# Hybrid encoder trunk: token-side sums in two portions, second product over all six blocks of a part

## Chip, cores, metric

One core of one Trainium2 chip runs the whole program. The metric is the device time of one execution in microseconds; the figure compared is the median over the runs of a kernel. The engines are named as in the profile: PE (matmul), PEld (its weight loads), DVE (VectorE), ACT (ScalarE), POOL (GpSimd) and SP, whose queue issues the loads.

## What is computed

Two layers of an encoder over 512 tokens with 1024 channels, in float32. Each layer runs a half-step feed-forward block, a mixer, a cross attention and a second half-step feed-forward block, each added to the residual x. The change touches only the feed-forward block, which therefore runs four times:

```
def swiglu(x, w_in, w_out):            # w_in 1024 x 5632, w_out 2816 x 1024
    gate, up = jnp.split(x @ w_in, 2, axis=-1)
    return (jax.nn.silu(gate) * up) @ w_out
...
x = x + 0.5 * swiglu(rms_norm(x, norm_ffn1[l]), ffn1_wi[l], ffn1_wo[l])
```

## The kernel before

Channels lie on the 128 partitions and the 512 tokens (T) along a row, so x is eight tiles of 128x512 (called x, or xs later in the program). Precision is kept by writing every matmul operand as a high and a low part: `split` makes the high part on ACT (an ACTIVATE copy) and the low part on DVE (source minus high), and `mm3` issues three matmuls, hi·hi, hi·lo and lo·hi. Names ending in hi and lo are such pairs: h (the normed input), w (weights of a plain product), s (weights of a Strassen-like product), t (sums of the input over tokens), f (hidden values).

The function `ffn` walks over 22 blocks f of 128 hidden channels. They are grouped by PARTS into four parts: f = 0 to 3, 4 to 9, 10 to 15 and 16 to 21.

- `plain(f)` (f = 0 to 3) makes gate and up with 24 matmuls of 512 columns each, into the PSUM tiles pg and pu. Its weights come through two `raw` buffers and three `whi`/`wlo` buffers of 512 columns; one such half feeds 12 matmuls.
- `seven(f)` (f from 4) makes the same with seven products of 12 matmuls of 256 columns, into PSUM tiles named p. In the order of issue they are 1, 2, 6, 3, 7, 5, 4. Products 1, 2 and 3 use h; 6, 7, 5 and 4 use sums of h over token halves and channel halves. The weight side needs sums of its own, made on DVE (`ws`), then split into `shi`/`slo` (seven buffers).
- `token_sums` makes the token-side sums once per feed-forward block, before any `seven`: for each of four channel pairs k one scaled copy on ACT (b), four DVE instructions on 256 columns (s), and two splits (thi on ACT, tlo on DVE).
- `second(f0, f1, ...)` is the second product (@ w_out) of a part that is finished: for each of eight output tiles, 12 or 18 matmuls of 512 columns into `po`, then two DVE instructions that add it to x. Its weights are loaded into `wr` and split into the same `whi`/`wlo` buffers. It is a generator and is advanced from inside the next part: each of the seven yields of a `seven` adds WO_RATE to a credit that starts at minus WO_LEAD, and each whole credit advances `second` by one step (24 steps for the first part, 32 for a later one). What is left is run at the end of the part. The last part's second product runs alone.

The order on each engine is made by a scheduler that follows program order where it can but lets an instruction go ahead when, by its own planning, an earlier one is not ready. After that each engine runs its instructions strictly in the order given.

Of the kernel before, what the change touches and what calls it, by code (L numbers as in the profile page):

```python
# [8 lines left out]
F32 = mybir.dt.float32  # L9
# [5 lines left out]
P = 128  # L15
# [15 lines left out]
REL_MAX = 256  # L31
LEAD, DENSE_RATE, ATT_RATE = 15, (1.0, 0.61, 0.98), 0.65
TURN_RATE = (0.5, 0.9)
PARTS, PLAIN, WO_RATE, WO_LEAD = (0, 4, 10, 16, 22), 4, 1.0, 4

PAR = {}
_n = 0
# [17 lines left out]
def trunk(tc, I, out, depth=DEPTH):  # L55
    nc = tc.nc
    ctx = ExitStack()
    with ctx:
# [13 lines left out]
        def stt(o, a, s, b, op0, op1):  # L72
            nc.vector.scalar_tensor_tensor(out=o, in0=a, scalar=s, in1=b, op0=op0, op1=op1)  # L73

        def act(o, i, f, **k):
            nc.scalar.activation(out=o, in_=i, func=f, **k)  # L76
# [4 lines left out]
        def t2(name, shape=None, dt=F32):  # L81
            return tp.tile(shape or [P, T], dt, tag="t", name=name, bufs=8)
# [45 lines left out]
        def pc(l, n, j=0):  # L128
            o, w = PAR[n]
            return par[:, l, o + j:o + j + 1]  # L130
# [10 lines left out]
        def split(o_hi, o_lo, src):  # L141
            act(o_hi, src, AF.Copy)
            tt(o_lo, src, o_hi.bitcast(F32), sub)
# [123 lines left out]
        def ffn(l, which):  # L267
            h = norm(l, f"norm_{which}")
            wi, wo = I[f"{which}_wi"][l], I[f"{which}_wo"][l]
            with tc.tile_pool(name="hid", bufs=1) as hidp:  # L270
# [10 lines left out]
                def plain(f):  # L281
                    nonlocal r
                    pg = bank(ROT[2 * f % 8], "pg")
                    proj(pg, wi[2 * f], KD, h)
                    pu = bank(ROT[(2 * f + 1) % 8], "pu")
                    proj(pu, wi[2 * f + 1], KD, h)
                    if f == 0:
                        if which == "ffn1" and l == 0:
                            for k in range(KD):
                                square_in(k)  # L290
                        r, _ = rstd(tag="po")
                    z = t2("z")
                    tt(z, pg, r, mult)
                    act(z, z, AF.Silu)
                    u = t2("u")
                    tt(u, pu, z, mult)
                    out(z, u)
# [1 line left out]

                sums = []  # L300

                def token_sums():
                    for k in range(4):
                        ga, gb = pc(l, f"norm_{which}", k), pc(l, f"norm_{which}", k + 4)
                        xa, xb = x[k], x[k + 4]
                        b1 = t2("b1")
                        act(b1, xa, AF.Copy, scale=ga)
                        s1, s2 = t2("s12"), t2("s34")
                        stt(s1[:, :Q], xa[:, Q:], ga, b1[:, :Q], mult, sub)
                        stt(s1[:, Q:], xb[:, Q:], gb, s1[:, :Q], mult, sub)  # L310
                        stt(s2[:, :Q], xb[:, Q:], gb, b1[:, Q:], mult, sub)
                        stt(s2[:, Q:], xb[:, :Q], gb, s1[:, Q:], mult, sub)
                        for s in (s1, s2):
                            hi = hidp.tile([P, T], F32R, name=f"thi{len(sums)}")
                            lo = hidp.tile([P, T], F32R, name=f"tlo{len(sums)}")
                            split(hi, lo, s)
                            sums.append((hi, lo))
                    hidp.tile([P, 72], F32, name="gap")

                def quarter(n):  # L320

# [80 lines left out]
                def second(f0, f1, last, tags):  # L402

                    for m in range(KD):
                        p = bank(tags[m % len(tags)], "po")
                        for g0 in range(f0, f1, 4):
                            n = min(4, f1 - g0)
                            raw = b2("wr")
                            nc.sync.dma_start(out=raw[:, :n * P], in_=wo[m][:, g0:g0 + n].rearrange("p k m -> p (k m)"))
                            hi = wp.tile([P, 512], F32R, tag="whi", name="whi", bufs=3)  # L410
                            lo = wp.tile([P, 512], F32R, tag="wlo", name="wlo", bufs=3)
                            split(hi[:, :n * P], lo[:, :n * P], raw[:, :n * P])
                            for k in range(n):
                                s = slice(k * P, k * P + P)
                                mm3(p, (hi[:, s], lo[:, s]), hid[g0 + k], g0 + k == f0, g0 + k == f1 - 1)
                                if k % 2:
                                    yield
                        t = t2("po")
                        stt(t, p, 0.5, r, mult, mult)
                        tt(x[m], x[m], t, add)  # L420
                        if last:
                            if which == "ffn1":
                                nc.sync.dma_start(out=x_dram[m], in_=x[m])
                            square_in(m)
                        yield

                wos, credit = iter(()), 0
                for f0, f1 in zip(PARTS, PARTS[1:]):
                    for f in range(f0, f1):
                        if f < PLAIN:  # L430
                            plain(f)
                            if f == 0:
                                token_sums()
                            continue
                        for _ in seven(f):
                            credit += WO_RATE
                            while credit >= 1:
                                credit -= 1
                                next(wos, None)
                    for _ in wos:  # L440
                        pass
                    wos, credit = second(f0, f1, f1 == KF, ("po", "ch") if f1 < KF else ROT[4:] + ROT[:4]), -WO_LEAD
# [689 lines left out]
        for l in range(depth):  # L1132
            ffn(l, "ffn1")
            mixer(l)
            cross(l)
            ffn(l, "ffn2")
# [94 lines left out]
```

## Time and profile before

| | us |
|---|---|
| median of 3 runs | 2468.22 |
| lowest and highest run | 2466.38, 2468.84 |
| profiled execution | 2472.44 |
| its span, first to last instruction | 2470.6 |
| PE busy in the span | 2395.3 (97%) |
| DVE busy in the span | 1868.7 (76%) |
| ACT busy in the span | 1145.8 (46%) |

Busy time of PE counts matmuls from start to modelled end, and they overlap, so 97% does not say that PE issues at its peak; what matters is the time between two starts. The feed-forward blocks begin at about 7, 876, 1234 and 2106 us of the span. In the views, L70 is the line of `tt` (a DVE or POOL tensor_tensor), L73 that of `stt`, L76 that of `act` and L79 that of `mm`, so instructions are told apart by their tiles, not by their lines.

### The profile page before, as it was taken

The page shows a single profiled execution, that of the slowest core. Times are in us where ns is not written, and L with a number is a line of the kernel's source. Part 1 is how long each engine was busy: PE and PEld are TensorE (multiplying, and loading weights), DVE is VectorE, ACT ScalarE, POOL GpSimd, SP SyncE. Part 2 cuts the span into 40 slices and gives each one's busy share as a digit, 9 for nine tenths or more (in the row PEclk, how much of TensorE's full clock was granted, in tenths as well). Part 3 has the DMA queues.
Part 4 walks back from the last instruction along what each step waited for, and adds up shares of the span by engine and source line. Part 5 has one row for each costly group of instructions (what it writes and reads, how often), then busy time and mean ns, then how long its engine had stood idle before and what let it go on. Part 6 is the DMA issues. An engine that isn't in the chain of part 4 may idle for free.

```text
span 2470.6 us, 42406 instructions
## 1 busy us (share of the span) xinstructions
PE 2395.3 (97%) x16650; PEld 2067.8 (84%) x16650; DVE 1868.7 (76%) x3417; ACT 1145.8 (46%) x2168; POOL 188.4 (8%) x246
## 2 busy tenths in 40 slices
PE   7999999999999999999989999999999999999999
PEld 5999987787689879899879999867876898798997
DVE  6888976767575658988868988767676756689887
ACT  5444444434465554444454444444444655544443
POOL 1000002111120000000100000121012101000001
PEclk9999999999999999999999999999999999999999
DMA  4233332210243223233322333322102423232332
GB/s 144 92 101 94 108 106 100 76 42 25 71 141 101 88 90 97 90 105 104 98 90 86 107 101 100 115 73 69 45 25 88 137 84 97 85 99 90 99 107 86
DMA packets 90968, 225.72 MB, mean 91 GB/s; under 512 B 10224, under 2 KB 27536, under 8 KB 90768
## 3 DMA queue, kind: packets, MB, share of 16 engines
q1 hardware_dynamic: 90768, 223.01, 28.3%
q8 instruction: 131, 2.15, 0.4%
q14 instruction: 69, 0.57, 0.1%
HBM read 215.89 MB, written 7.08 MB: 90 GB/s over the span
## 4 chain that ended last, share of the span: by engine, by line
PE 86%; DVE 7%; issue 2%; DMA 2%; ACT 2%; POOL 0%; POOLq 0%; ACTq 0%; DVEq 0%; SPq 0%
PE p L79 29%; PE po L79 19%; PE pxq L79 5%; PE pin L79 4%; PE pxw L79 3%; PE pu L79 3%; PE pg L79 3%; PE pqk L79 3%; PE pout L79 3%; DVE wlo L70 1%; PE pbvf L79 1%; PE pf L79 1%; PE ptt L79 1%; DVE s L73 1%; DMA raw<-in_x_wv_dram 1%
## 5 line engine op out<-in xcount | busy, mean ns | idle before, releaser
L79 PE MATMUL p<-thi,shi 128*128 128x256 f32 x1152 | 326.8, 285 | 6.8 <-ACT shi L76 6.7
L70 DVE TENSOR_TENSOR wlo<-raw,whi 128x512 fp32r<-128x512 f32 (+3 forms) x326 | 229.6, 713 | 133.6 <-ACT whi L76 124.0
L79 PE MATMUL p<-tlo,shi 128*128 128x256 f32 x1152 | 323.3, 282 | 0.0
L79 PE MATMUL p<-thi,slo 128*128 128x256 f32 x1152 | 322.0, 282 | 0.0
L76 ACT ACTIVATE whi<-raw 128x512 fp32r<-128x512 f32 (+3 forms) x326 | 195.0, 604 | 247.5 <-PE pin L79 49.3
L79 PE MATMUL po<-flo,whi 128*128 128x512 f32 x704 | 277.0, 393 | 0.0
L79 PE MATMUL po<-fhi,wlo 128*128 128x512 f32 x704 | 276.0, 393 | 0.0
L79 PE MATMUL po<-fhi,whi 128*128 128x512 f32 x704 | 274.8, 394 | 0.1
L79 PE MATMUL p<-hhi,shi 128*128 128x256 f32 x864 | 244.4, 283 | 0.1
L79 PE MATMUL p<-hhi,slo 128*128 128x256 f32 x864 | 243.9, 282 | 0.0
L79 PE MATMUL p<-hlo,shi 128*128 128x256 f32 x864 | 242.9, 281 | 0.0
L79 PEld LDWEIGHTS p<-thi,shi 128*128 128x128 f32 x1152 | 217.5, 189 | 28.7 <-ACT shi L76 22.4
L76 ACT ACTIVATE whi<-wr 128x512 fp32r<-128x512 f32 x224 | 119.6, 535 | 251.6 <-PE po L79 146.9
L76 ACT ACTIVATE shi<-ws 128x512 fp32r<-128x512 f32 x288 | 173.1, 629 | 106.7 <-DVE ws L70 103.5
L79 PEld LDWEIGHTS p<-tlo,shi 128*128 128x128 f32 x1152 | 217.4, 189 | 4.8
L79 PEld LDWEIGHTS p<-thi,slo 128*128 128x128 f32 x1152 | 216.1, 189 | 5.2 <-DVE slo L70 1.6
L70 DVE TENSOR_TENSOR slo<-ws,shi 128x512 fp32r<-128x512 f32 x288 | 188.2, 684 | 4.2 <-ACT shi L76 3.7
L70 DVE TENSOR_TENSOR wlo<-wr,whi 128x512 fp32r<-128x512 f32 x224 | 132.1, 590 | 69.0 <-ACT whi L76 69.0
L76 ACT ACTIVATE shi<-raw 128x512 fp32r<-128x512 f32 x216 | 127.9, 624 | 97.3 <-DMA raw<-in_ffn_wi_dram 97.0
L70 POOL TENSOR_TENSOR ssa<-ssa,sq 128x512 f32<-128x512 f32 x63 | 85.8, 1362 | 1100.3 <-ACT sq L76 1099.8
L79 PEld LDWEIGHTS p<-hhi,shi 128*128 128x128 f32 x864 | 163.4, 189 | 7.2 <-ACT shi L76 2.9
L79 PEld LDWEIGHTS p<-hlo,shi 128*128 128x128 f32 x864 | 163.6, 189 | 4.9
(341 smaller groups left out, 5781.9 us busy)
## 6 DMA issues: line engine op xcount, KB each, us to landing
raw<-in_ffn_wi_dram SPq DMA_DIRECT2D x175, 512.0 KB, 3.3
wr<-in_ffn_wo_dram SPq DMA_DIRECT2D x128, 256.0 KB, 2.7
raw<-in_w_in_dram SPq DMA_DIRECT2D x30, 512.0 KB, 3.4
wr<-in_ffn_wo_dram SPq DMA_DIRECT2D x96, 128.0 KB, 2.3
raw<-in_x_wk_dram SPq DMA_DIRECT2D x16, 512.0 KB, 3.8
raw<-in_x_wv_dram SPq DMA_DIRECT2D x16, 512.0 KB, 4.0
raw<-in_x_wq_dram SPq DMA_DIRECT2D x16, 512.0 KB, 3.7
raw<-in_w_qk_dram SPq DMA_DIRECT2D x12, 512.0 KB, 3.8
```

The source lines that it names most:

```text
L70: (eng or nc.vector).tensor_tensor(out=o, in0=a, in1=b, op=op)
L73: nc.vector.scalar_tensor_tensor(out=o, in0=a, scalar=s, in1=b, op0=op0, op1=op1)
L76: nc.scalar.activation(out=o, in_=i, func=f, **k)
L79: nc.tensor.matmul(o, lhsT=w, rhs=x, start=start, stop=stop)
```

## The change

Two things change. `token_sums` takes a list of channel pairs and is called twice, with pairs 0 and 1 after the block f = 1 and with pairs 2 and 3 after f = 2, instead of once with all four after f = 0. And the second product is advanced by 0.85 steps per yield from a credit of -2, instead of 1.0 from -4. By the arithmetic of the credits the 32 steps of a later part needed 36 of the 42 yields and now need 40; the 24 steps of the first part needed 28 and now need 31. The number of instructions is the same on every engine, and outside the feed-forward blocks their order is the same too.

```
-PARTS, PLAIN, WO_RATE, WO_LEAD = (0, 4, 10, 16, 22), 4, 1.0, 4
+PARTS, PLAIN, WO_RATE, WO_LEAD = (0, 4, 10, 16, 22), 4, 0.85, 2
...
-                def token_sums():
-                    for k in range(4):
+                def token_sums(ks):
+                    for k in ks:
...
-                    hidp.tile([P, 72], F32, name="gap")
+                    if 3 in ks:
+                        hidp.tile([P, 72], F32, name="gap")
...
                             plain(f)
-                            if f == 0:
-                                token_sums()
+                            token_sums({1: (0, 1), 2: (2, 3)}.get(f, ()))
                             continue
```

DVE, first feed-forward block, from the last weight split of block f = 1 on (`wlo<-raw`, the eighth of 16 such halves); the numbers behind s, b, thi and tlo tell the tiles apart. Before:

```order
L70 TENSOR_TENSOR wlo<-raw,whi 128x512
L70 TENSOR_TENSOR u<-pu,z 128x512
L73 SCALAR_TENSOR_TENSOR s_258<-x,par,b_256 128x256
L73 SCALAR_TENSOR_TENSOR s_259<-x,par,b_256 128x256
L73 SCALAR_TENSOR_TENSOR s_258<-x,par,s_258 128x256
L70 TENSOR_TENSOR flo<-u,fhi 128x512
L73 SCALAR_TENSOR_TENSOR s_259<-x,par,s_258 128x256
L73 SCALAR_TENSOR_TENSOR s_274<-x,par,b_272 128x256
L70 TENSOR_TENSOR tlo_265<-s_258,thi_264 128x512
L73 SCALAR_TENSOR_TENSOR s_274<-x,par,s_274 128x256
```

The same place after:

```order
L70 TENSOR_TENSOR wlo<-raw,whi 128x512
L70 TENSOR_TENSOR u<-pu,z 128x512
L70 TENSOR_TENSOR z<-pg,rstd 128x512
L70 TENSOR_TENSOR wlo<-raw,whi 128x512
L70 TENSOR_TENSOR flo<-u,fhi 128x512
L70 TENSOR_TENSOR wlo<-raw,whi 128x512
L70 TENSOR_TENSOR u<-pu,z 128x512
L70 TENSOR_TENSOR wlo<-raw,whi 128x512
L73 SCALAR_TENSOR_TENSOR s_337<-x,par,b_335 128x256
L70 TENSOR_TENSOR flo<-u,fhi 128x512
```

Before, 24 instructions of the sums stand between the eighth and the ninth `wlo`, with only u, flo and one z among them; after, the ninth to the eleventh `wlo` stand ahead of the first sum.

DVE, second portion of the sums (after block f = 2, same feed-forward block), from the last of the four instructions on its first pair to the last `wlo` of a plain block, the sixteenth. After:

```order
L73 SCALAR_TENSOR_TENSOR s_449<-x,par,s_448 128x256
L70 TENSOR_TENSOR slo<-raw,shi 128x512
L70 TENSOR_TENSOR tlo_455<-s_448,thi_454 128x512
L73 SCALAR_TENSOR_TENSOR s_464<-x,par,b_462 128x256
L70 TENSOR_TENSOR tlo_459<-s_449,thi_458 128x512
L73 SCALAR_TENSOR_TENSOR s_464<-x,par,s_464 128x256
L73 SCALAR_TENSOR_TENSOR s_465<-x,par,b_462 128x256
L73 SCALAR_TENSOR_TENSOR s_465<-x,par,s_464 128x256
L70 TENSOR_TENSOR tlo_471<-s_464,thi_470 128x512
L70 TENSOR_TENSOR wlo<-raw,whi 128x512
```

Between the fifteenth and the sixteenth `wlo` there are now eight instructions on 256 columns (three of them and flo stand ahead of the rows shown) and one flo, one slo and three tlo on 512. Before, only one flo and two slo stood between those two.

On PE the matmuls of the second product (po) stand between those of the seven products (84 matmuls p per block). Counted from the program's order, po matmuls inside each block f = 4 to 21, and behind the last:

```
f        4  5  6  7  8  9 | 10 11 12 13 14 15 | 16 17 18 19 20 21 | behind
before  12 24 30 30 16 11 |  6  9 30 36 30 14 | 10 24 30 36 30 14 | 136
after   12 24 24 24 16 11 | 11 16 30 18 30 24 | 18 24 30 18 30 24 | 144
```

Ahead of a block's product 6 stand its products 1 and 2 (24 matmuls p) and some po matmuls: in f = 10 and f = 11 three each before, four each after.

DVE at the handover from block f = 10 to f = 11, first feed-forward block: the tail of a block (z, u, z) and the weight sums of the next (ws). The second ws is the operand of product 6. Before:

```order
L70 TENSOR_TENSOR z<-p_1720,v 128x256
L70 TENSOR_TENSOR u<-p_1720,v 128x2x256
L70 TENSOR_TENSOR z<-z,rstd 128x512
L70 TENSOR_TENSOR ws<-raw 128x512
L70 TENSOR_TENSOR wlo<-wr,whi 128x256
L70 TENSOR_TENSOR u<-u,z 128x512
L70 TENSOR_TENSOR ws<-ws,raw 128x512
```

After:

```order
L70 TENSOR_TENSOR z<-p_1726,v 128x256
L70 TENSOR_TENSOR u<-p_1726,v 128x2x256
L70 TENSOR_TENSOR z<-z,rstd 128x512
L70 TENSOR_TENSOR ws<-raw 128x512
L70 TENSOR_TENSOR ws<-ws,raw 128x512
```

A split of the second product's weights and one u stood between the two ws of f = 11; now nothing does.

## Prediction

> **What bounds the kernel now.** I read the page first, then who PE waited for, then the chain of work around the largest of these waits, then the granted clock there.
>
> ```profile
> PE 2395.3 (97%) x16650; PEld 2067.8 (84%) x16650; DVE 1868.7 (76%) x3417; ACT 1145.8 (46%) x2168; POOL 188.4 (8%) x246
> PE 86%; DVE 7%; issue 2%; DMA 2%; ACT 2%; POOL 0%; POOLq 0%; ACTq 0%; DVEq 0%; SPq 0%
> ```
>
> The second line is the chain that ended last: PE holds 86% of it, so a faster kernel must either issue fewer matmuls (the change does not) or let PE wait less. DVE's 7% is where PE stood behind DVE. The waits of PE say where:
>
> ```profile
> PE pg L79 <- DVE wlo L70: 22.5, 4, 6.8
> ...
> PE p L79 <- ACT shi L76: 6.7, 8, 1.4
> ```
>
> Columns: total us, times, longest. The first row is one wait in each of the four feed-forward blocks, in a plain block, for a low weight part. Why DVE was late there is in the chain of the second feed-forward block (start, us, what):
>
> ```profile
> 894.81 0.57 DVE wlo L70
> ...
> 895.43 0.88 DVE s L73 x2
> ...
> 907.19 0.68 DVE tlo L70
> 907.87 0.61 DVE wlo L70
> 908.48 0.04 issue
> 908.53 3.86 PE pg L79 x10
> 912.39 5.00 PE pu L79 x22
> 917.39 5.44 PE pg L79 x24
> ```
>
> DVE makes a wlo at 894.81, then all the token sums, and the next wlo only at 907.87; nothing on PE needs those sums yet. PE has three halves of weights at most, uses them up and stands. The last row gives PE's price: 5.44/24 = 0.227 us per matmul of 512 columns. The clock adds to the wait. Windows laid on the stretches where the granted clock fell (length, PE busy, clock, DMA share, GB/s), the first and last of six, and the sum:
>
> ```profile
> 44.40:51.20 6.80, 3.85 (x9) 0.50 0.21 76
> ...
> 2266.40:2269.80 3.40, 3.40 (x19) 0.51 0.40 151
> sum 30.60, PE 23.07; mean PE 3.85
> ```
>
> The first four windows (44.4, 907.9, 1266.3, 2136.7) begin inside or right behind the four waits for wlo; the last two (177.5 and 2266.4) are 3.40 us each and begin behind a wait for shi. Work done at half clock takes twice its time, so half of the busy 23.07 is lost: (23.07 - 6.80)/2 = 8.1 us behind the waits for wlo and 3.4 us behind those for shi.
>
> [...]
>
> **The sums in two portions.** Price of the sums on DVE, from the stretch 894.7 to 908.4 and from successive starts (start, duration):
>
> ```profile
> L70 DVE TENSOR_TENSOR tlo<-s,thi 128x512 fp32r<-128x512 f32 x8 | 5.5, 684 | 0.0
> L73 DVE SCALAR_TENSOR_TENSOR s<-xs,par,s 128x256 f32<-128x256 f32 x8 | 3.8, 479 | 0.0
> L73 DVE SCALAR_TENSOR_TENSOR s<-xs,par,b 128x256 f32<-128x256 f32 x8 | 3.7, 480 | 0.0
> ...
> 897.62 0.48 DVE L73 SCALAR_TENSOR_TENSOR s<-xs,par,s 128x256 f32<-128x256 f32 x1
> 898.02 0.69 DVE L70 TENSOR_TENSOR tlo<-s,thi 128x512 fp32r<-128x512 f32 x1
> 898.62 0.48 DVE L73 SCALAR_TENSOR_TENSOR s<-xs,par,s 128x256 f32<-128x256 f32 x1
> ```
>
> Durations overlap; by starts an instruction on 256 columns takes 0.40 and one on 512 takes 0.60 us. All sums: 16 x 0.40 + 8 x 0.60 = 11.2 us; a portion 5.6. A plain block keeps PE for 48 x 0.227 = 10.9 us and DVE for four wlo, z, u and flo, 7 x 0.60 = 4.2. So 4.2 + 5.6 = 9.8 fits into each of the blocks f = 2 and f = 3, where 4.2 + 11.2 did not fit behind f = 0. DVE is not short of time over the whole stretch either (PE, PEld, DVE, ACT, POOL busy):
>
> ```profile
> 889.00:931.00 42.00, 36.76 (x172) 30.59 (x171) 28.61 (x53) 22.51 (x36) 0.00 (x0) 0.96 0.25 75
> ```
>
> 13 of 42 us were idle, mostly behind the sums; this is the cover.
>
> Does a hole remain? In the new order the widest distance between two wlo is the one from the fifteenth to the sixteenth: eight instructions of 0.40, and flo, slo, three tlo and the wlo itself at 0.60: 6.8 us. Let U be the end of the up product of f = 2. DVE does u (U + 0.7) and the fifteenth wlo (U + 1.3), then these 6.8: the sixteenth is there at U + 8.1. PE runs the gate product of f = 3 (5.44) and the first half of its up product (2.72) and needs the sixteenth wlo with the third matmul after: U + 8.6. It just fits, by 0.5 us, if nothing else is waited for. Two things are: the ACT copies thi, in step with DVE, and, newly ahead of that wlo in DVE's queue, an slo of f = 4, which waits for a load:
>
> ```profile
> raw<-in_ffn_wi_dram SPq DMA_DIRECT2D x5, 512.0 KB, 3.4
> ```
>
> Its buffer is free when the fourteenth wlo is done, about 1 us before U; on SP the loads of the plain blocks stand directly behind each other, so it lands at U + 2.5, is split by ACT by U + 3.1, and DVE reaches the slo at about U + 3.7. Hidden, with 0.6 us to spare. I take 0.5 us of new waiting per feed-forward block, 2.0 in all: nearest to the case just worked out. The ends are 0, and one portion wholly uncovered: 4 x 5.6 = 22.4.
>
> The sums are first needed by product 6 of f = 4. The second portion ends at U + 9.3 (tlo behind the last wlo: + 0.60, and a z), PE reaches product 6 at U + 10.9 + 24 x 0.118 = U + 13.7. Hidden, unless DVE is 4 us late. ACT's twelve instructions move along and are hidden: 22.51 busy of 42. The dummy tile costs nothing; it issues no instruction.
>
> So the waits for wlo go: 22.5 + 8.1 - 2.0 = 28.6 us.
>
> **The second product over six blocks.** It moves matmuls, not their number. What it can win is the row of shi. The chain at the handovers f = 9 to 10 and 10 to 11, second feed-forward block:
>
> ```profile
> 928.27 2.84 PE p L79 x24
> ...
> 1013.35 3.80 PE p L79 x32
> 1017.18 0.42 DVE z L70
> ...
> 1018.80 0.62 DVE ws L70
> 1019.44 0.70 DVE ws L70
> ...
> 1020.24 0.64 ACT shi L76
> 1020.93 0.51 PE p L79 x2
> ...
> 1029.40 0.42 DVE z L70
> ...
> 1031.62 0.34 DVE wlo L70
> 1031.96 0.61 DVE u L70
> ...
> 1034.32 0.50 PE p L79 x2
> ```
>
> From the end of a block's product 4, DVE must do z, u, z, ws, ws and ACT a shi before PE can start the next block's product 6: 1020.93 - 1017.18 = 3.75 us. Where wlo and u stand between the two ws it is 1034.32 - 1029.40 = 4.92. PE covers this with products 1 and 2, 24 x 0.118 = 2.84 us, and the po matmuls that stand there: three, 0.68. Of that 3.52 about 0.16 is gone before DVE sees the end (a matmul of 256 columns lasts 0.28 and is issued every 0.118). Waits: 3.75 - 3.36 = 0.4 and 4.92 - 3.36 = 1.6. In the new order both handovers have the short chain and four po matmuls (cover 3.59): 0.2 each; f = 9 has five: none. The total in this region, by counting matmuls p and po in a window from f = 9 to f = 11:
>
> ```profile
> 139.49:176.82 37.33, 31.51 (x252) 30.39 (x251) 7.19 (x12) 0.87 (x3) 1.00 0.30 100
> ...
> 2228.38:2265.72 37.34, 31.50 (x253) 30.37 (x252) 7.20 (x12) 0.89 (x3) 1.00 0.32 100
> ...
> 2228.38:2265.72 37.34, 6.07 (x20) 3.33 (x20) 0.00 (x0) 1.00 0.32 100
> ```
>
> 253 x 0.118 + 20 x 0.227 = 34.4 of 37.3 us: 2.9 lost, alike in the first and the fourth feed-forward block. In the new order I leave 0.7 (0.4 for the two waits, 0.3 for gaps behind them): 2.2 x 4 = 8.8 us won, and the 3.4 us of half clock with them, by the row. Bounds: 0 if the handovers stay as they are, 4 x 2.9 + 3.4 = 15.0. The blocks that lose po matmuls (36 to 18 at f = 13 and 19) keep six ahead of product 6, cover 4.2 - 0.16 against 3.75: no wait. The eight po matmuls more behind the last block are issued without a wait as the 136 before: no cost. SP's loads of wr and raw alternate more often; a raw load now sits behind a wr load that waits for its buffer, which I cost at nothing because raw is loaded for the block after; without that cover it is the third rival's size.
>
> **Sum.** 28.6 + 8.8 + 3.4 = 40.8 us off the profiled execution's 2472.44. The median of the runs, 2468.22, lies 4.2 lower and loses the same: 2427.4.
>
> **Rivals.**
> 1. The second portion is late (an slo that waits for its load, or thi in step with DVE): PE waits about 2 us for the sixteenth wlo in each feed-forward block and pays one half-clock stretch, 1.7 us: 4 x 3.7 - 2.0 = 12.8 less: 2440. For it: the margin of 0.5 us. Against: 13 us of idle DVE.
> [...]
> 2. The handovers do not improve (waits move to other blocks): 8.8 + 3.4 less: 2440. For it: four po matmuls are still short of the 3.75. Against: the long chain of 4.92 is gone from f = 11.
> 3. Slower: the two portions and f = 4's weight sums, all on DVE, collide at the step from plain blocks to products, and with raw released later the loads follow late. DVE has 13 us idle there; if in-order waits use none of it, all 11.2 us stand on the path, with 8.1/4 = 2.0 us of half clock, 13.2 in place of (22.5 + 8.1)/4 = 7.65 per feed-forward block: 4 x 5.6 = 22 slower, 2490. It decides from 10.2 us of new waits per feed-forward block, which is 40.8/4. Against: both portions fit their blocks.
> 4. The change does not do what it says: the sums still ahead of wlo, about 2468. The new order speaks against it: three wlo stand ahead of the first sum.
>
> **Chances.** Forecast (2420 to 2434) 0.60; rival 1, 0.14; rival 2, 0.14; both, about 2450, 0.04; rival 4 or gains lost elsewhere, 0.03; slower, 0.05. A measurement here tells about 0.2%, 5 us, from no change. Range: low end 22.5 + 8.1 + 15.0 = 45.6 less, with a little for the small waits at other handovers, 2420; high end past both 2440 cases, 2447. Faster 0.92, same 0.03, slower 0.05.
>
> **What would show it.** Right: the row of pg waiting for wlo falls from 22.5 to under 3; no half clock at the plain blocks; the chain there is PE alone; the window f = 9 to 11 loses under 1 us. Wrong: a wait for the sixteenth wlo (pu), for tlo in product 6, for shi in f = 4, or p waiting for raw's load; or the same rows of shi in other blocks.

## The result, and the profile after

| | before | after |
|---|---|---|
| median of 4 runs each, same chip, us | 2468.07 | 2428.24 |
| lowest and highest run | 2466.38, 2468.84 | 2425.09, 2429.79 |
| profiled execution, its span | 2472.44, 2470.6 | 2425.09, 2423.3 |
| the four feed-forward blocks, first pg to last po | 369.8, 357.7, 360.6, 360.3: 1448.4 | 356.5, 348.9, 351.6, 347.4: 1404.4 |

The ratio is 0.9838 [0.9821, 0.9855], 39.8 us by the medians. The profiled executions lie 47.3 apart, because the one before is 4.4 above its median and the one after 3.1 below. 44.0 of these 47.3 are in the four feed-forward blocks (last line of the table, from the first and the last start of these tiles' matmuls), the part of the program that the change is in. Not all of them are the change's: the profile before has a stretch of 3.4 us at half clock at 20.5 us (granted clock 0.50), ahead of anything that the change moves, where the two profiles of the kernel after have a clock of 1.00. I take it for chance; with the work at half clock counted as double it is 1.7 of the 44.0.

The page of the kernel after, in the same lines as shown of before (busy time, share and instructions of each engine, then the chain that ended last):

```profile
PE 2376.5 (98%) x16650; PEld 2057.7 (85%) x16650; DVE 1871.4 (77%) x3417; ACT 1142.0 (47%) x2168; POOL 188.9 (8%) x246
PE 89%; DVE 5%; issue 2%; DMA 2%; ACT 1%; POOL 0%; POOLq 0%; ACTq 0%; SPq 0%; DVEq 0%
```

The instruction counts are the same. PE's share of the chain went from 86% to 89%, DVE's from 7% to 5%. What PE waited for (total us, times, longest):

```profile
PE p L79 <- ACT shi L76: 2.0, 2, 1.0
...
PE pg L79 <- DVE wlo L70: 1.5, 2, 1.3
```

The 22.5 us of pg behind wlo are 1.5, and these two waits stand at the very start of the third feed-forward block, not behind the sums (more of them below). Of the eight waits for shi two are left. The chain through the plain blocks of the second feed-forward block (start, us, what), the place where DVE's row of sums stood in the prediction:

```profile
880.38 5.44 PE pu L79 x24
885.82 5.44 PE pg L79 x24
891.25 5.44 PE pu L79 x24
896.70 5.44 PE pg L79 x24
902.13 5.45 PE pu L79 x24
907.58 2.84 PE p L79 x24
910.42 1.40 PE po L79 x6
911.82 0.26 PE p L79 x2
```

PE alone, each product of 24 matmuls in 5.44 us: it never waits, and it goes into product 6 of f = 4 (the last row) without a wait. (In the first feed-forward block it waits there for 1.0 us; that is one of the two waits for shi.) The stretch around these blocks before (length, then PE, PEld, DVE, ACT, POOL busy, granted clock, DMA share, GB/s):

```profile
900.00:935.00 35.00, 29.76 (x144) 24.80 (x143) 25.38 (x45) 17.46 (x30) 0.00 (x0) 0.95 0.31 93
```

and after:

```profile
885.00:920.00 35.00, 35.00 (x194) 30.32 (x193) 32.29 (x59) 21.12 (x37) 0.00 (x0) 1.00 0.35 113
```

The clock is 1.00 where it was 0.95, and PE is busy for all of the 35.0 us where it was for 29.8. (The numbers of matmuls cannot be compared, as the window after reaches further into the products, whose matmuls are short.) DVE is busy for 32.3 us where it was for 25.4.

### The profile page after: what moved, and what is told of

Its sections match the earlier page's. It is cut to its first block, busy times and chain, and to the rows that moved or that the text cites. A ratio compares the mean times of both kernels' runs of the same rounds, so it can differ in the third digit from the quotient of the medians.

```text
span 2423.3 us, 42438 instructions
## 1 busy us (share of the span) xinstructions
PE 2376.5 (98%) x16650; PEld 2057.7 (85%) x16650; DVE 1871.4 (77%) x3417; ACT 1142.0 (47%) x2168; POOL 188.9 (8%) x246
## 4 chain that ended last, share of the span: by engine, by line
PE 89%; DVE 5%; issue 2%; DMA 2%; ACT 1%; POOL 0%; POOLq 0%; ACTq 0%; SPq 0%; DVEq 0%
PE p L79 29%; PE po L79 18%; PE pxq L79 5%; PE pin L79 4%; PE pu L79 4%; PE pxw L79 3%; PE pout L79 3%; PE pg L79 3%; PE pqk L79 3%; DVE wlo L70 1%; PE pbvf L79 1%; PE pf L79 1%; PE ptt L79 1%; PE pr L79 1%; PE pxs L79 1%
## 5 line engine op out<-in xcount | busy, mean ns | idle before, releaser
L70 DVE TENSOR_TENSOR wlo<-wr,whi 128x512 fp32r<-128x512 f32 x224 | 142.2, 642 | 54.8 <-ACT whi L76 54.1
L76 ACT ACTIVATE z<-z 128x512 f32<-128x512 f32 x88 | 55.5, 631 | 258.4 <-DVE z L70 258.4
```

Of the source, the lines that this page charges most:

```text
L70: (eng or nc.vector).tensor_tensor(out=o, in0=a, in1=b, op=op)
```

## Experiments

All were run beside the kernel before on the same chip, and each ratio is to it. "FFN" is the length of the four feed-forward blocks in the profiled execution, as in the table above; since the rest of the program moves by a few us from execution to execution, it shows a small effect better than the median does. It is one execution each all the same: the two of the kernel after differ by 2.0, and one stretch at half clock more or less is 1.7.

| kernel | median | before, same chip | ratio | FFN |
|---|---|---|---|---|
| after | 2428.24 | 2468.07 | 0.9838 [0.9821, 0.9855] | 1404.4 |
| after, second time | 2432.57 | 2470.47 | 0.9848 [0.9820, 0.9875] | 1406.4 |
| sums alone | 2443.92 | 2472.09 | 0.9884 [0.9864, 0.9903] | 1419.6 |
| second product alone | 2456.97 | 2472.09 | 0.9937 [0.9924, 0.9950] | 1436.1 |
| all sums behind f = 2 | 2449.54 | 2472.09 | 0.9911 [0.9897, 0.9924] | 1426.9 |
| portions behind f = 0, 1 | 2435.10 | 2472.09 | 0.9848 [0.9834, 0.9862] | 1411.8 |
| portions behind f = 2, 3 | 2435.00 | 2470.47 | 0.9856 [0.9834, 0.9878] | 1414.5 |
| second product at 2 steps a yield | 2461.93 | 2470.36 | 0.9973 [0.9960, 0.9986] | 1446.8 |
| after, third raw buffer | 2416.68 | 2470.47 | 0.9784 [0.9762, 0.9805] | 1404.0 |
| after, four wr buffers | 2430.09 | 2470.47 | 0.9838 [0.9816, 0.9860] | 1407.6 |
| before, third raw buffer | 2456.50 | 2470.36 | 0.9941 [0.9919, 0.9963] | 1447.1 |

**The two halves of the change.** The sums alone, against after:

```
-PARTS, PLAIN, WO_RATE, WO_LEAD = (0, 4, 10, 16, 22), 4, 0.85, 2
+PARTS, PLAIN, WO_RATE, WO_LEAD = (0, 4, 10, 16, 22), 4, 1.0, 4
```

> Only the token sums in two portions (after f = 1 and f = 2); the second product keeps rate 1.0 and lead 4. My sum: the waits for wlo go with their half clock, 28.6 us off, 2439 (2435 to 2443); the row of pg waiting for wlo falls from 22.5 to under 3; the row of p waiting for shi stays near 6.7. Rival (the second product carries the gain): within 5 us of 2468.

The second product alone, against before:

```
-PARTS, PLAIN, WO_RATE, WO_LEAD = (0, 4, 10, 16, 22), 4, 1.0, 4
+PARTS, PLAIN, WO_RATE, WO_LEAD = (0, 4, 10, 16, 22), 4, 0.85, 2
```

> Only the second product's rate and lead (0.85, -2); all token sums stay after f = 0. My sum: 8.8 us of handover waits and 3.4 us of half clock go, 2456 (2454 to 2460); the row of pg waiting for wlo stays near 22.5. [...] Rival (handover waits only move to other blocks): 2468. Rival (it carries most of the gain): below 2445.

The sums alone take 28.2 us off for 28.6 expected (the median lies just above the stated range because the kernel before was 4 us slower on this chip). The second product alone takes 15.1 off (12.4 to 18.8 by its interval), where 12.2 were expected, 8.8 for the waits and 3.4 for the half clock at the handovers. The interval leaves out the 8.8 alone. Together the two would make 43.3, and the whole change measured 39.8 (35.8 to 44.2). By FFN it is 28.8 and 12.3, together 41.1, against 44.0. So the halves add up within what is measured. Each removes its own row of waits. Waits of PE in the kernel with the sums alone:

```profile
PE p L79 <- ACT shi L76: 8.4, 11, 1.4
...
PE pu L79 <- DVE wlo L70: 1.6, 2, 0.9
```

and in the one with the second product alone:

```profile
PE pg L79 <- DVE wlo L70: 24.0, 6, 6.8
```

The first keeps the waits for shi (11 of them for 8) and has lost those for wlo behind the sums; the second keeps the waits for wlo, and its list has no row of p waiting for shi.

**How long a stretch without wlo does PE cover?** All sums in one portion, behind f = 2:

```
-                            token_sums({1: (0, 1), 2: (2, 3)}.get(f, ()))
+                            token_sums({2: (0, 1, 2, 3)}.get(f, ()))
```

> All four channel pairs in one portion after f = 2, second product as in the changed kernel. DVE has 11.8 us between the fifteenth and the sixteenth wlo, where the kernel before had 13.6 and waited 5.4. My theory (the length of the stretch without a wlo decides): a wait of about 3.6 us per feed-forward block and 1.7 to 2.0 us of half clock behind it, 2428 + 4 x 5.5 = 2450 (2442 to 2454). Rival (it was the place right behind block 0 that hurt, not the size of the portion): 2428.

```profile
PE pu L79 <- DVE wlo L70: 15.9, 5, 4.0
```

One wait of 3.7 to 4.0 us in each feed-forward block (the fifth of the row, 0.7, stands at the start of the first block in the kernel before too); 3.6 were expected, and 2449.54 for 2450. The wait is shorter than the 5.2 of before (6.8 in the first block), with the same sums in one piece, because the way from wlo to wlo is shorter: in the second feed-forward block 11.8 us (902.17 to 913.95) for 13.0 (894.81 to 907.79). The order has put the last tlo behind the wlo, and no z stands among the sums. A window of 6 us laid behind the third of the four waits (columns as above, PE alone):

```profile
1272.00:1278.00 6.00, 5.51 (x16) 0.50 0.48 160
```

Half clock follows, behind all four: in windows of 6 us behind the other three the clock is 0.72. The two portions one block earlier, behind f = 0 and f = 1:

```
-                            token_sums({1: (0, 1), 2: (2, 3)}.get(f, ()))
+                            token_sums({0: (0, 1), 1: (2, 3)}.get(f, ()))
```

> Two portions, one block earlier than in the changed kernel: after f = 0 and after f = 1. The longest stretch without a wlo is 8.0 us, and PE's cover in the kernel before was 13.6 - 5.4 = 8.2. My theory: no wait, 2428 (2425 to 2432). Rival (behind block 0 any portion hurts): one wait of 1 to 3 us per feed-forward block with half clock, 2435 to 2447.

```profile
PE pg L79 <- DVE wlo L70: 3.4, 6, 1.3
...
PE pu L79 <- DVE wlo L70: 2.6, 4, 0.7
```

Neither forecast is met as it stands. "No wait" is missed: the waits for wlo are ten small ones, 6.0 us, where the kernel after has three, 2.2 us (1.5 of pg and 0.7 of pu), and FFN is 5.4 to 7.4 longer than in the two profiles of after. The rival's 1 to 3 us with half clock are missed too: behind the sums they are 0.2 to 1.2, and the granted clock of the whole execution is 0.997, where the two of after have 0.998 and 0.996. The ratio equals that of after's second measurement, so the medians do not tell the two apart. What wins is that there are two portions; which of these blocks they stand behind is worth a few us at most.

**Is the rival that forecast a collision at the step to the products priced rightly?** The portions one block later, behind f = 2 and f = 3:

```
-                            token_sums({1: (0, 1), 2: (2, 3)}.get(f, ()))
+                            token_sums({2: (0, 1), 3: (2, 3)}.get(f, ()))
```

> Two portions, one block later than in the changed kernel: after f = 2 and after f = 3, second product as in the changed kernel. The longest stretch without a wlo is 5.2 us: no wait for wlo. But 14.4 us of DVE work instead of 7.8 stand ahead of the first slo made from a weight sum, the operand of product 6 of f = 4. My theory: PE waits about 6 us at product 6 in each feed-forward block, with about 2 us of half clock, 2428 + 4 x 8 = 2460 (2448 to 2466) against 2468 before; the row is p waiting for shi, slo or tlo. Rival (products 1 and 2 and the second product cover it): 2428.

A miss: 2435.00, 2.4 above after's second run on this chip and not some 27; FFN is 8.1 longer, and the rest of that execution shorter. PE's waits, and PE's instructions at the step to product 6 of f = 4 in the second feed-forward block (start, duration, what; in brackets the wait and what ended it):

```profile
PE p L79 <- ACT shi L76: 5.2, 6, 1.1
...
PE p L79 <- DVE slo L70: 1.3, 4, 0.4
```

```profile
917.49 0.39 PE L79 MATMUL po<-fhi,wlo 128*128 128x512 f32 x1
918.95 0.39 PE L79 MATMUL p<-thi,shi 128*128 128x256 f32 x1 [1.08 <-ACT shi L76]
...
919.75 0.38 PE L79 MATMUL p<-thi,slo 128*128 128x256 f32 x1 [0.29 <-DVE slo L70]
```

PE waits 1.08 and 0.29 us here, and as long in the other three blocks, where 6 were expected. The rival came nearest: products 1 and 2 and the second product cover most of it. I had counted DVE's work alone. In the order of this kernel 24 po matmuls of the first part stand ahead of product 6 of f = 4, where the kernel after has six; 18 x 0.227 = 4.1 us of cover that I had not put in. What a late sum costs is what is left after the other matmuls that the planner places in front of its user.

**Is it the place of the po matmuls that makes the handovers?** The second product crowded into the front of a part, against after:

```
-PARTS, PLAIN, WO_RATE, WO_LEAD = (0, 4, 10, 16, 22), 4, 0.85, 2
+PARTS, PLAIN, WO_RATE, WO_LEAD = (0, 4, 10, 16, 22), 4, 2.0, 2
```

> The changed kernel with the second product bunched instead of spread: 2.0 steps per yield, lead 2; sums in two portions as in the changed kernel. By the handover arithmetic (the operand of product 6 comes 3.75 us, or 0.6 us more for each DVE instruction of 512 columns put between, behind the end of a block; cover is 24 matmuls p and the po matmuls ahead of product 6, less 0.16) two blocks have no po at all and seven have three or four: the waits sum to 2.9 us per feed-forward block where the changed kernel has 0.03 by the same arithmetic, and about 0.3 of gaps behind each of nine waits: 4 x 5.6 = 22 us slower than the changed kernel with some half clock not counted (14 to 28 slower; ratio to before about 0.992). The row of p waiting for shi rises from 2 to above 10. Rival (the po matmuls' place does not matter; the gain of spreading was something else): no slower than the changed kernel.

```profile
PE p L79 <- ACT shi L76: 12.1, 25, 1.0
...
PE p L79 <- DVE slo L70: 5.3, 9, 0.8
...
PE po L79 <- ACT fhi L76: 2.1, 4, 0.5
```

The ratio of 0.9973 against 0.9848 makes it 31 us slower than after, most of what the change had won; 22 were expected, 14 to 28. The direction holds: handovers without po matmuls wait, 25 times in place of 2. The size was missed because I counted waits for shi alone. Those for slo (5.3) and for fhi (2.1) came with them; the three rows make 19.5 us, where the kernel after has 2.0. The granted clock of this profiled execution is 0.992, where the two of after have 0.998 and 0.996. What is missing from 1.0 makes 19.7 us of its span, against 4.8 and 9.7 in those two; by this estimate half clock cost it another 10 to 15.

**What are the two waits that are left?** They lie in the first feed-forward block at f = 4 and in the second at f = 11. The chain there (first block; start, us, what):

```profile
57.05 4.64 DMA raw<-in_ffn_wi_dram
...
64.25 0.64 ACT shi L76
...
64.94 0.50 PE p L79 x2
```

The kernel after was run a second time to see whether they are chance. 

> The changed kernel once more, beside the others on this chip: ratio 0.9838 to the kernel before, within its interval (0.982 to 0.986). Waits of about 1.1 us for shi in single places, where a load of raw landed late, stand in other places than in the first profile if the landing is chance, in the same places if the order makes it.

```profile
1001.20 4.38 DMA raw<-in_ffn_wi_dram
...
1011.88 0.50 PE p L79 x2
```

Both waits come again, behind the same loads (in the first profile the second of them starts at 1000.20 and takes 4.37). So the order makes them, and not chance. A raw load takes 3.3 us in the median and took 4.4 to 4.7 there, and it could not start earlier, because it waits for one of two raw buffers. SP's own waits in the first profile show that (L117 is the line of the raw loads, and the first of a block's ws reads raw):

```profile
SPq L117 <- DVE ws L70: 497.1, 71, 10.7
```

Slow loads alone do not make a wait: in the first profile ten of 177 take 4.36 us or more, and of the eight of these that are issued after the first 10 us only these two cost PE something. Why a load is slow is open. The next kernel gives raw a third buffer, and pays for it in SBUF with two of the six buffers of the tag that wr uses:

```
-            return bp.tile([P, T], F32, tag="b", name=name, bufs=6)
+            return bp.tile([P, T], F32, tag="b", name=name, bufs=4)
...
-            raw = wp.tile([P, 1024], F32, tag="raw", name="raw", bufs=2)
+            raw = wp.tile([P, 1024], F32, tag="raw", name="raw", bufs=3)
```

> The changed kernel with three raw buffers instead of two, paid with four instead of six buffers for wr (the tag b). A raw load is issued a block's half earlier, so a late landing has cover. My theory: the single waits of 1.1 us for shi and the loads of the cross attention's weights on the chain go; 2 to 4 us off in the feed-forward blocks, 5 to 20 elsewhere: 2405 to 2422. Rival (four wr buffers cost more than they free, or the load itself bounds): 2428 or slower.

The control takes the two wr buffers away and nothing else:

> Control: only the four instead of six buffers of the tag b, two raw buffers as before. If the wr buffers were cover that nothing needs: 2428 within 3. If they were needed: slower by 4 us or more, and the third raw buffer's own worth is the difference to its kernel.

With the third buffer it is 2416.68, 15.9 below the second run of after on the same chip and inside the expected range; it beats both kernels. The control, 2430.09, is no slower than after, so giving those two buffers up costs nothing. (It has the first of the two waits, with 1.8 us, and not the second.) ACT's longest rows of waits for loads of raw in the feed-forward blocks and in the cross attention, in the second profile of after:

```profile
ACT shi L76 <- DMA raw<-in_ffn_wi_dram: 88.5, 58, 3.1
...
ACT whi L76 <- DMA raw<-in_x_wv_dram: 14.7, 8, 2.5
```

In the kernel with the third buffer no row of ACT waiting for raw is left, and PE's list has no row of p waiting for shi. The load itself is no faster: the issues of raw read the same in both, with 3.3 us to landing.

```profile
raw<-in_ffn_wi_dram SPq DMA_DIRECT2D x175, 512.0 KB, 3.3
```

So it is the earlier start that counts. Little of the 15.9 lies where I looked: by the first and last matmuls of the stages, FFN is 2.4 shorter (1406.4 to 1404.0), the two cross attentions 6.7 (173.0 to 169.5 and 172.7 to 169.5) and the two mixers 5.2. Of these only the cross attentions are safe: the first profile of after has nearly the same FFN (1404.4) and mixers as short as with the third buffer, and its cross attentions are the longer ones again. The rest of the 15.9 is not placed. That the waits of ACT for raw cost PE nothing in most of the feed-forward blocks, and something in stages with less cover, is my reading of this and was not tried by itself.

Last, whether the third buffer and the change compete for the same us: the same two lines on the kernel before.

> The kernel before with three raw buffers and four of the tag b, to see what the third buffer is worth without the change. My theory: the waits for wlo behind the token sums stay (22.5, they are DVE's), the handover waits stay (the DVE chain makes them, not the load); the gain is that of the third buffer in the changed kernel, 14 us, mostly in the cross attention: 2455 to 2460. Rival (a late raw load made the waits of the kernel before): 2440 or less.

```profile
PE pg L79 <- DVE wlo L70: 22.5, 4, 6.8
PE p L79 <- ACT shi L76: 6.9, 8, 1.4
```

13.9 off (2470.36 to 2456.50), as expected, and the two rows of waits that the change removes stand as they were. Within the scatter the two add up: 13.9 without the change (9.1 to 20.0 by its interval), 15.9 with it.

## Why the prediction was right

It said 2427.4; measured were 2428.24 and, on another chip, a ratio of 0.9848. That the number came within 1 us is luck: the interval alone runs from 35.8 to 44.2 us off, and two terms put at nothing measured about 2 us each. What bears it are the rows of waits, which went as it said. By the terms:

- **Waits for wlo, 28.6.** The sums alone took 28.2 by the medians and 28.8 by FFN, the latter with up to 1.7 from the stretch at 20.5 us in the profile before. The step that carried it was the comparison of the longest distance between two wlo on DVE with the three halves that PE has in hand. DVE around the end U of the up product of f = 2 (second feed-forward block after, U = 896.70; start, duration):

```profile
897.34 0.68 DVE L70 TENSOR_TENSOR wlo<-raw,whi 128x512 fp32r<-128x512 f32 x1
...
900.15 0.69 DVE L70 TENSOR_TENSOR slo<-raw,shi 128x512 fp32r<-128x512 f32 x1
...
904.15 0.69 DVE L70 TENSOR_TENSOR wlo<-raw,whi 128x512 fp32r<-128x512 f32 x1
904.75 0.69 DVE L70 TENSOR_TENSOR tlo<-s,thi 128x512 fp32r<-128x512 f32 x1
```

  The sixteenth wlo ends at 904.84, U + 8.1, as worked out; slo begins at U + 3.45, worked out was U + 3.7; the portion ends at U + 8.7 for U + 9.3. The margin of 0.5 us held in all four feed-forward blocks, and rival 1 did not come.
- **The 2.0 us left for new waits** had a wrong cause and, by luck, a fitting size. Nothing was lost at the sixteenth wlo. What came in its place were two waits of 1.0 behind raw loads.
- **The handovers, 8.8 + 3.4.** The second product alone took 12.3 off FFN and 15.1 (12.4 to 18.8) off the median. The chain at f = 10 and f = 11 after (third feed-forward block):

```profile
1349.04 0.93 PE po L79 x4
1349.96 0.02 issue
1349.98 0.51 PE p L79 x2
...
1361.83 0.94 PE po L79 x4
1362.77 0.50 PE p L79 x2
```

  Four po matmuls, then product 6 (p x2) after 0.02 us or none; 0.2 was forecast. Rival 2 did not come. Its argument was that four po matmuls are short of the 3.75 us; here they are short by 0.02 at most. (The wait of 1.0 at f = 11 in the second block is the one behind the raw load.)
- **The half clock behind short pauses.** The prediction let the 3.4 us go with the row of shi. They stand in its windows at 177.5 and 2266.4, behind the longest pause at the handovers of the first and the fourth feed-forward block. Windows of 5 us behind the same pause in the other two (columns as above, PE alone):

```profile
1034.00:1039.00 5.00, 4.66 (x34) 1.00 0.32 104
1395.00:1400.00 5.00, 4.79 (x35) 1.00 0.29 105
```

  Two of four alike pauses, of 1.4 us each, were followed by half clock (0.66 in windows of 5 us behind the first and the fourth). The kernel before with the third raw buffer has the same four pauses, and again two were followed (0.66 behind the third and the fourth, 1.00 behind the others); with the sums alone it was one of four (0.66 behind the first, 1.00 behind the others). That is 5 of 12. Windows of 3.41 us around the four pauses of before:

```profile
174.07:177.48 3.41, 1.97 (x12) 1.00 0.14 38
1030.82:1034.23 3.41, 2.07 (x16) 1.00 0.13 38
1392.63:1396.04 3.41, 1.97 (x12) 1.00 0.14 38
2263.03:2266.44 3.41, 1.97 (x12) 1.00 0.14 38
```

  PE was busy for 1.97 us in three of them and for 2.07 in the one around the second pause; the first and the fourth pause were followed, the third, with the same 1.97, and the second were not. What decides this was not shown. In the kernel after, without the pauses, no window of 5 us, laid end to end from the first feed-forward block's start to its end and likewise through the other three, has a clock below 0.99. So the term was right in its sign, but it is a chance of about 40% for each pause and not a price: 12 pauses cost 5 x 1.7 us, 0.7 each or 2.8 an execution, where the profiled execution happened to have 3.4.
- **The loads of raw "at nothing".** This step failed: a term of nothing measured 2 us in the two waits, and they go when the buffer is added (FFN's 2.4 less is hardly more than the 2.0 between the two profiles of after). The cover that I named (raw is loaded for the block after) was there, but two buffers made the load start late, and a slow load of 4.4 to 4.7 us used the cover up.
- **The po matmuls behind the last block "no cost".** This failed too, and by about as much. Behind a feed-forward block the next stage's first wlo stands on DVE behind what is left of the second product, and the order there is another one than before (so the order outside the feed-forward blocks is the same but for their first few us). PE at the start of the mixers, before and then after:

```profile
PE pin L79 <- DVE wlo L70: 0.4, 1, 0.4
PE pin L79 <- DVE wlo L70: 3.1, 4, 1.4
```

  With the 1.5 us of pg behind wlo at the start of the third block, and less the waits for hhi that were there before (1.2 and 0.7), this makes about 2 us more. The kernel with the second product alone has these rows (3.2 and the 1.5), the one with the sums alone has neither.
- **Rival 3, 2490,** was overpriced. With the portions later still its collision did happen and cost 8.1 by FFN, 2.4 by the medians, since the order puts po matmuls in front. Nothing in the traces brings it near the 40.8 at which it would have decided.

## What to carry to other kernels

Where an engine runs its queue in order, look for the longest row of instructions on it that nobody needs yet, and compare that row with what the waiting engine has in hand: three buffers of 2.72 us here cover 8.2 us; a way of 13.0 us from wlo to wlo cost 5.2, one of 11.8 cost 3.7 and one of 6.8 nothing. Before pricing a late operand, look at what the order puts in front of its user, not only at the engine that makes it. And look for buffers that can be spared: two of them, given up for a third one for the loads that wait, were worth more than a third of the whole change.

## What the runs showed of the hardware

In the profile before, the stretches at half clock in the feed-forward blocks start at 20.47, 44.36, 177.48, 907.93, 1266.33, 2136.73 and 2266.44 us. Those at 44.36, 1266.33 and 2136.73 last 6.83 us, the other four 3.41, and the granted clock in each is 0.50. Two matmuls in a row start 0.213 us apart there for 0.118 on 256 columns, and 0.426 for 0.227 on 512. By this a stretch of 3.41 us that is full of matmuls cost 1.5 to 1.6 us; the 1.7 in the prediction and above counts the work at half clock as double, which is a little too much.

How often a pause of PE was followed by such a stretch: behind the sums, all eight of 3.7 us or more in the windows (four before, 5.2 to 6.8 us; four with all sums behind f = 2, 3.7 to 4.0). Of the 12 pauses of 1.4 us (1.8 from start to start of the matmuls around), 5. Of the two pauses of 1.0 us behind the raw loads in the kernel after, none: the windows there have a clock of 1.00.
